# Turning q and k of eight attention heads by VectorE blocks and 128-byte load pieces instead of by TensorE transposes

## The chip, the cores and the metric

One core of a Trainium2 chip runs the whole program. The metric is the device time of one execution in microseconds (us). Five engines work in parallel, each with its own in-order queue: TensorE (PE; its weight loads are shown apart as PEld), VectorE (DVE), ScalarE (ACT), GpSimd (POOL) and SyncE (SP). SP and POOL issue most of the DMA transfers.

## The reference

One layer over 512 tokens of width 1024 in fp32: an RMS norm, one input projection, three token mixers (pooling, a gated linear recurrence "RG-LRU", and stick-breaking attention with 8 heads of 128), gates, a merge, an output projection, and a SwiGLU feed-forward block. Cut to what the change touches:

```python
h = rms_norm(x, norm_mix)
u_pool, u_lru, q, k, v, g_logits = jnp.split(h @ w_in, splits, axis=-1)

# RG-LRU gates, xb = the convolved u_lru in 16 blocks of 64
r = sigmoid(einsum('bshi,hij->bshj', xb, w_rg) + b_rg)
i = sigmoid(einsum('bshi,hij->bshj', xb, w_ig) + b_ig)

# attention: norm over each head's 128 columns, then scores
qh = rms_norm(q.reshape(B, S, 8, 128), q_norm)   # y * rsqrt(mean(y*y) + EPS) * g
kh = rms_norm(k.reshape(B, S, 8, 128), k_norm)
for each block of 128 queries (end = its last row):
    z = einsum('bqhd,bkhd->bhqk', qh_block, kh[:, :end]) * 128 ** -0.5
    log_keep = where(causal, log_sigmoid(-z), 0)
    after = reverse_cumsum(log_keep) - log_keep
    w = where(causal, exp(log_sigmoid(z) + after), 0)
    y = einsum('bhqk,bkhd->bqhd', w, vh[:, :end])
```

## The kernel before

**Products.** Every fp32 product runs as three fp32r passes on PE: high part times high part, high times low, low times high (`mm3`, L304 to 308; `product`, L310 to 317, in a seven-product scheme). A weight tile of 128x1024 is loaded as `raw` (or `qw`), ACT copies it to its high part `whi` (L141), and DVE subtracts to get the low part `wlo` (L142). There are three buffers each for raw, whi and wlo, and SP's next weight load (L148) waits until the wlo of an older raw is done. PE starts a 512-column matmul about every 0.21 us.

**Order.** The program is written as stages with side tasks between the products (`step`, `tick`, and the list `bg`), and a scheduler sets each engine's queue from the order in the code, from raised priorities (`tc.high_priority`) and from explicit places (`tc.issue_after`). Each engine then works through its queue in that order.

**Stages.** In time: the RMS norm and the first gates; the LRU's products with convolution, gates and scan in four chunks, beside more gates; the v, k and q products (`tok_product`, L828 its matmuls); the gates of the third branch; the pool chunks with the attention heads as side tasks; the branch projections, the merge, the output projection, the feed-forward block.

**LRU gates.** For each chunk c, `conv` builds xc, `split` writes its high part xch and its low part xcl (L650), and `gates(0)`, `gates(1)` run three passes each into one PSUM tile `lg`: xch with the high weights lwh, xcl with lwh, xch with the low weights lwl (L660). Each pass is a pair of matmuls on 64 rows.

**q, k, v.** The products leave blocks of 256 tokens by 512 columns: `snap` copies PSUM to an SBUF tile r (ACT, L841), `final` adds the second product (DVE, L849), and `post` ends the block. For q and k, ACT squares the 128x1024 tile (L788, L794) and DVE sums each 128 columns (L789, L795); q's sums go to `qss` and are used as scales of the scores later; k's sums become a reciprocal root `krs`, and `post2` scales r with it in eight ACT steps (L807). `store` (POOL's DMA, L781) puts the block into a DRAM tensor qd.

**Heads.** `head_tasks(h)` gives eight tasks. `load` (SP, L1068) fetches q, k and v of the head into `at` tiles, 128 partitions (tokens) x 4 x 128, as 512-byte pieces. `trans` turns q and k so that the head's 128 columns lie on partitions: four PE transposes each into a PSUM tile `pq` (L1075), from which ACT writes the high part `qkh` (L1079), DVE the low part `qkl` (L1080), and ACT an fp32 copy `f` of the first 128 (L1083). `scores` makes z in three groups; the first 128x128 block is one fp32 product of the two f (L1101), the others are `mm3`. Sigmoids (K, A on ACT), a scan (DVE), transposes of the weights w (`wtrans`, PE, tile `pw`) and the product with v (`yout`, tile `py`) follow.

Of the kernel before, what the change touches and what calls it, by code (L numbers as in the profile page):

```python
# [64 lines left out]
def layer_kernel(ctx: ExitStack, tc: tile.TileContext, x, xt, vecs, w_in, w_qkv7, w_gate7, w_pool, w_rg, w_ig,  # L65
# [371 lines left out]
    with ExitStack() as first:  # L437
# [131 lines left out]
        def lru_constants():  # L569
            dve.tensor_scalar(qg, vcol("q_norm"), QSCALE, None, ALU.mult)  # L570
# [58 lines left out]
        def lru_chunk(c):  # L629
# [17 lines left out]
            def split():  # L647
                st["h"], st["l"] = b4([2, S], f"xch{c}", "b", F32R), b4([2, S], f"xcl{c}", "b", F32R)
                dve.tensor_copy(st["h"], xc)
                dve.tensor_tensor(st["l"], xc, st["h"].bitcast(F32), ALU.subtract)  # L650
# [3 lines left out]
            def gates(j):  # L654
                ct = 2 * c + j
                ps = pb.tile([P, 2, S], F32, tag="mm", name=f"lg{c}{j}")
                for n, (w, x_) in enumerate((("h", "h"), ("h", "l"), ("l", "h"))):
                    for n2 in range(2):
                        q = LH[n2]
                        nc.tensor.matmul(ps[:, n2, :], lw[w][q, ct, :], il(st[x_][q, j, :]),  # L660
                                         start=n == 0, stop=n == 2)
                for n2 in range(2):
                    q, o = LH[n2], LH[1 - n2]
                    act(two(st["r"][q, j, :]), in_order(ps[q, n2, :]), AF.Tanh, scale=0.5, bias=brg[q, ct:ct + 1])
                    act(two(st["i"][q, j, :]), in_order(ps[o, n2, :]), AF.Tanh, scale=0.5, bias=bigx[o, ct:ct + 1])

            def tanh():
                st["t"] = b4([2, S], f"lt{c}")
                dve.scalar_tensor_tensor(st["i"], st["i"], 1.0, xc, ALU.add, ALU.mult)
# [9 lines left out]
            def both():  # L679
                gates(0)  # L680
                gates(1)

            return lambda: early(conv), lambda: early(split), both, tanh
# [68 lines left out]
        def step(*fs):  # L752
            bg.append(lambda: [f() for f in fs])
# [3 lines left out]

        c0, s0, g0, t0 = lru_chunk(0)
# [8 lines left out]
        step(c3), step(s3), step(of(lru_decay, 1), of(lru_scan, 0)), step(t2, of(lru_input, 1))  # L767
# [16 lines left out]
        def post(t, i, j, r):  # L784
            if t < 2:
                sq = b4([2, 512], f"sq{t}{i}{j}")
                if t == 0:
                    act(sq, r, AF.Square)  # L788
                    dve.tensor_reduce(qss[:, 2 * j:2 * j + 2, 4 * i:4 * i + 4],  # L789
                                      sq.rearrange("p a (b d) -> p a b d", d=HD), AX.X, ALU.add)  # L790
                    store(t, i, j, r)
                    return
# [5 lines left out]
            if t == 2:  # L798
                store(t, i, j, r)
# [966 lines left out]
```

## Time and profile before

| what | value |
|---|---|
| three runs | 866.56, 866.76, 868.84 us; median 866.76 |
| the profiled execution | 866.14 us, span 864.3 us, granted clock 0.999 |
| PE / PEld busy | 857.8 / 788.8 us |
| DVE / ACT / POOL busy | 732.3 / 527.0 / 88.8 us |
| DMA packets | 116643, of these 8160 under 512 bytes |

The span is the time between the first and the last instruction of the execution. Busy time is summed per engine; a row of the groups shows the line of the code, the engine, the output and input tiles, the shape, how many, the busy time in us, the mean of one in ns, and the idle time before it with what ended it. SPq is SP's own queue, where DMA issues are counted.

### The profile page before, as it was taken

To read this page: it belongs to the slowest core of one execution; us is meant where nothing else is said; L and a number is where in the kernel's file an instruction comes from. 1 tells how busy PE (TensorE), PEld (TensorE's weight loads), DVE (VectorE), ACT (ScalarE), POOL (GpSimd) and SP (SyncE) were. 2 spreads that over 40 slices of the span, in tenths; PEclk is the share of its full clock that TensorE was granted. 3 is DMA by queue.
4 is the path that set the end of the run, shared out by engine and by line. 5 is a ranking of instruction groups with operands and counts; after the bars stand their busy time and mean duration, and the time that the engine had idled before them with its cause. 6 is when DMAs were issued, how large, how long until landed. Compare 5 with 4: busy or idle time off the path is not lost.

```text
span 864.3 us, 14239 instructions
## 1 busy us (share of the span) xinstructions
PE 857.8 (99%) x5547; PEld 788.8 (91%) x5547; DVE 732.3 (85%) x937; ACT 527.0 (61%) x751; POOL 88.8 (10%) x128
## 2 busy tenths in 40 slices
PE   9999999999999999999999999999999999999998
PEld 7888878888899988889989988889999999999998
DVE  7899897998796598967897787699988888899974
ACT  7554989556966567556665545465555555755642
POOL 1110002132432101000001100000000000121200
PEclk9999999999999999999999999999999999999999
DMA  9586346799592766745737955345533433798913
GB/s 336 169 287 206 101 152 186 224 319 264 172 306 83 234 205 213 226 118 157 242 93 176 200 167 177 100 140 141 163 105 98 123 98 125 224 243 206 192 38 122
DMA packets 116643, 154.08 MB, mean 178 GB/s; under 512 B 8160, under 2 KB 90080, under 8 KB 116576
## 3 DMA queue, kind: packets, MB, share of 16 engines
q1 hardware_dynamic: 103904, 107.30, 39.1%
q0 software_dynamic: 12528, 45.62, 22.4%
q8 instruction: 43, 0.70, 0.3%
q10 hardware_dynamic: 144, 0.26, 0.1%
q14 instruction: 24, 0.20, 0.1%
HBM read 132.71 MB, written 18.87 MB: 175 GB/s over the span
## 4 chain that ended last, share of the span: by engine, by line
PE 92%; ACT 4%; DVE 2%; issue 1%; DMA 0%; SPq 0%; DVEq 0%; ACTq 0%
PE ps_y L315 11%; PE ps_q L828 8%; PE ps_x L315 8%; PE ps_dy L1685 6%; PE ps_dx L1685 5%; PE ps_br L308 3%; PE ps_br L306 3%; PE ps_br L307 3%; PE ps_gate L731 3%; PE ps_bY L1309 2%; PE ps_gy L315 2%; PE ps_bX L1309 2%; PE ps_gx L315 2%; PE ps_pool L306 2%; PE ps_pool L308 2%; PE ps_pool L307 2%
## 5 line engine op out<-in xcount | busy, mean ns | idle before, releaser
L141 ACT ACTIVATE whi<-raw 128x1024 fp32r<-128x1024 f32 x69 | 72.8, 1055 | 75.8 <-PE ps_out L307 16.0
L142 DVE TENSOR_TENSOR wlo<-raw,whi 128x1024 fp32r<-128x1024 f32 x69 | 84.2, 1220 | 25.8 <-ACT whi L141 25.1
L142 DVE TENSOR_TENSOR wlo<-qw,whi 128x1024 fp32r<-128x1024 f32 x48 | 58.4, 1219 | 16.5 <-ACT whi L141 16.5
L141 ACT ACTIVATE whi<-qw 128x1024 fp32r<-128x1024 f32 x48 | 50.3, 1052 | 26.2 <-PE ps_q L828 11.8
L1470 ACT ACTIVATE wh_S<-w_S 128x1024 fp32r<-128x1024 f32 x36 | 38.3, 1063 | 28.7 <-PE ps_y L315 20.1
L1591 POOL DMA_DIRECT2D dw<-in_w_down_dram x20 | 16.9, 862 | 305.1 <-DVE wl L1471 242.9
L1471 DVE TENSOR_TENSOR wl_S<-w_S,wh_S 128x1024 fp32r<-128x1024 f32 x36 | 43.8, 1219 | 3.3 <-ACT wh_S L1470 3.3
L1470 ACT ACTIVATE wh<-w 128x1024 fp32r<-128x1024 f32 x27 | 28.7, 1061 | 27.7 <-PE ps_x L315 9.4
L1471 DVE TENSOR_TENSOR wl<-w,wh 128x1024 fp32r<-128x1024 f32 x27 | 32.9, 1219 | 7.9 <-ACT wh L1470 7.9
L1470 ACT ACTIVATE whdS<-dw 128x1024 fp32r<-128x1024 f32 x20 | 21.3, 1064 | 20.9 <-PE ps_dy L1685 10.6
L1118 DVE TENSOR_TENSOR_SCAN E<-K,ahead 128x512 f32<-128x512 f32 (+3 forms) x32 | 25.3, 812 | 6.2 <-ACT K L1114 6.2
L1471 DVE TENSOR_TENSOR wldS<-dw,whdS 128x1024 fp32r<-128x1024 f32 x20 | 24.2, 1220 | 5.4 <-ACT whdS L1470 5.4
L306 PE MATMUL ps_br<-yph,whi 128*128 128x512 f32 x64 | 24.6, 385 | 0.0
L306 PE MATMUL ps_lru<-HH,whi 128*128 128x512 f32 x64 | 24.6, 384 | 0.0
L306 PE MATMUL ps_pool<-HH,whi 128*128 128x512 f32 x64 | 24.5, 383 | 0.0
L306 PE MATMUL ps_br<-yHH,whi 128*128 128x512 f32 x64 | 24.5, 383 | 0.0
L306 PE MATMUL ps_gate<-HH,whi 128*128 128x512 f32 x64 | 24.4, 381 | 0.0
L307 PE MATMUL ps_br<-yHL,whi 128*128 128x512 f32 x64 | 24.3, 379 | 0.0
L308 PE MATMUL ps_lru<-HH,wlo 128*128 128x512 f32 x64 | 24.3, 379 | 0.0
L307 PE MATMUL ps_gate<-HL,whi 128*128 128x512 f32 x64 | 24.3, 379 | 0.0
L307 PE MATMUL ps_pool<-HL,whi 128*128 128x512 f32 x64 | 24.3, 379 | 0.0
L308 PE MATMUL ps_pool<-HH,wlo 128*128 128x512 f32 x64 | 24.3, 379 | 0.0
(745 smaller groups left out, 3427.2 us busy)
## 6 DMA issues: line engine op xcount, KB each, us to landing
raw<-in_w_in_dram SPq DMA_DIRECT2D x31, 512.0 KB, 5.3
qw<-in_w_qkv_dram SPq DMA_DIRECT2D x24, 512.0 KB, 7.7
dw<-in_w_down_dram POOLq DMA_DIRECT2D x20, 512.0 KB, 8.5
w<-in_w_ffn_gate_dram SPq DMA_DIRECT2D x36, 256.0 KB, 4.0
w<-in_w_ffn_up_dram SPq DMA_DIRECT2D x36, 256.0 KB, 4.6
raw<-in_w_branch_dram SPq DMA_DIRECT2D x16, 512.0 KB, 4.1
qw<-in_w_qkv_dram POOLq DMA_DIRECT2D x12, 512.0 KB, 8.5
qd<-r POOLq DMA_DIRECT2D x12, 512.0 KB, 7.3
```

The costliest lines, as they stand in the source:

```text
L141: act(hi, raw, AF.Copy)
L142: los.append(dve.tensor_tensor(lo, raw, hi.bitcast(F32), ALU.subtract).ins)
L306: nc.tensor.matmul(ps, lh, rh, start=start, stop=False, skip_group_check=skip)
L307: nc.tensor.matmul(ps, lh, rl, start=False, stop=False, skip_group_check=skip)
L308: nc.tensor.matmul(ps, ll, rh, start=False, stop=stop, skip_group_check=skip)
L315: nc.tensor.matmul(o, a_[a][:, w, k, :], il2(b_[b][:, k, :]), start=first and n == k == 0, stop=last and n == 2 and k == 3, skip_group_che ...
L731: nc.tensor.matmul(pss[n // 2][n % 2], w[:, k % 2, n * P:(n + 1) * P], il(hu[k][x_]), start=k == 0 and w is wh and x_ == 0, stop=k == KT - ...
L828: nc.tensor.matmul(ps[:, a, :], b_[:, k, ts_], il(a_[:, kk, :]), start=first and n == k == 0, stop=n == 2 and k == 3, skip_group_check=True)
L1309: nc.tensor.matmul(o, ah[x_][:, w, k, :], il2(b[k][y_]), start=first_ and n == k == 0, stop=n == 2 and k == 3, skip_group_check=True)
L1470: act(h, src, AF.Copy)
L1471: dve.tensor_tensor(l, src, h.bitcast(F32), ALU.subtract)
L1685: nc.tensor.matmul(o, a_[a][:, w, k0 + k, :], il2(b_[b][:, k, :]), start=first and i == k == 0, stop=last and i == 2 and k == nk - 1, skip ...
```

## The change

- `turn`: DVE transposes each 128x1024 tile of q and k in 32x32 blocks (into the tile that held the squares), and that is stored. `load` fetches q and k of a head in four DMAs each; a DMA takes 512 pieces of 32 elements (128 bytes) and puts each block where the turned tile wants it. v is loaded as before. The PE transposes into pq and that tile are gone; `trans` reads the loaded tile.
- Squares: eight ACT operations of 128x128 with `accum_out` (each followed by reading the accumulator) in place of one of 128x1024 and DVE's sum.
- `k_norm` is folded into q's factor qg, so k needs no factor and its f is the loaded tile itself. The first block of z, and what reads it, is in plain instead of interleaved column order, as is the product with `wtf`. A tile "gap" and a wider f only move addresses.
- LRU gates: both PSUM tiles of a chunk are filled together, the passes that read xcl last. On DVE, `behind_lo(3)` puts chunk 3's xcl ahead of li and of `lru_input(1)`.
- q's block (1, 0) is finished later: its squares in the first part of the third branch's gates, its transpose and store in the second.

```diff
-            dve.tensor_scalar(qg, vcol("q_norm"), QSCALE, None, ALU.mult)
+            dve.scalar_tensor_tensor(qg, vcol("q_norm"), QSCALE, vcol("k_norm"), ALU.mult, ALU.mult)
...
-                dve.tensor_tensor(st["l"], xc, st["h"].bitcast(F32), ALU.subtract)
+                st["lo"] = dve.tensor_tensor(st["l"], xc, st["h"].bitcast(F32), ALU.subtract).ins
...
-            def gates(j):
-                ct = 2 * c + j
-                ps = pb.tile([P, 2, S], F32, tag="mm", name=f"lg{c}{j}")
-                for n, (w, x_) in enumerate((("h", "h"), ("h", "l"), ("l", "h"))):
+            def gates():
+                ps = [pb.tile([P, 2, S], F32, tag="mm", name=f"lg{c}{j}") for j in range(2)]
+                for js, passes in (((0, 1), (("h", "h", True, False), ("l", "h", False, False))),
+                                   ((0, 1), (("h", "l", False, True),))):
+                    for j in js:
+                        for w, x_, start, stop in passes:
+                            for q in LH:
+                                nc.tensor.matmul(ps[j][:, LH.index(q), :], lw[w][q, 2 * c + j, :],
+                                                 il(st[x_][q, j, :]), start=start, stop=stop)
+                for j in range(2):
...
-                dve.scalar_tensor_tensor(st["i"], st["i"], 1.0, xc, ALU.add, ALU.mult)
+                with behind_lo(3) if c == 2 else nullcontext():
+                    dve.scalar_tensor_tensor(st["i"], st["i"], 1.0, xc, ALU.add, ALU.mult)
...
+        def behind_lo(c):
+            return tc.issue_after(lru[c]["lo"])
...
+        def behind_input():
+            with behind_lo(3):
+                lru_input(1)
...
-        step(c3), step(s3), step(of(lru_decay, 1), of(lru_scan, 0)), step(t2, of(lru_input, 1))
+        step(c3), step(s3), step(of(lru_decay, 1), of(lru_scan, 0)), step(t2, behind_input)
...
         def post(t, i, j, r):
-            if t < 2:
-                sq = b4([2, 512], f"sq{t}{i}{j}")
-                if t == 0:
-                    act(sq, r, AF.Square)
-                    dve.tensor_reduce(qss[:, 2 * j:2 * j + 2, 4 * i:4 * i + 4],
-                                      sq.rearrange("p a (b d) -> p a b d", d=HD), AX.X, ALU.add)
-                    store(t, i, j, r)
-                    return
-                s_ = cst.tile([P, 8], F32, tag="ssq", name=f"ssq{t}{i}{j}", bufs=2)
-                act(sq, r, AF.Square)
-                dve.tensor_reduce(s_, sq.rearrange("p a (b d) -> p (a b) d", d=HD), AX.X, ALU.add)
-                dve.tensor_scalar(s_, s_, 1.0 / HD, EPS, ALU.mult, ALU.add)
-                bg.append(lambda: post2(t, i, j, r, s_))
             if t == 2:
                 store(t, i, j, r)
-
-        def post2(t, i, j, r, s_):
-            y = cst.tile([P, 8], F32, tag="krs", name=f"krs{i}{j}", bufs=2)
-            rsqrt(y.rearrange("p (a b) -> p a b", a=2), s_.rearrange("p (a b) -> p a b", a=2), (2, 4),
-                  f"q{t}{i}{j}")
-            v = r.rearrange("p a (b d) -> p (a b) d", d=HD)
-            for n in range(8):
-                act(v[:, n, :], v[:, n, :], AF.Copy, scale=y[:, n:n + 1])
-            store(t, i, j, r)
+                return
+            z = b4([2, 512], f"sq{t}{i}{j}")
+            sums = qss[:, 2 * j:2 * j + 2, 4 * i:4 * i + 4] if t == 0 else cst.tile(
+                [P, 2, 4], F32, tag="ssq", name=f"ssq{t}{i}{j}", bufs=2)
+            for a in range(2):
+                for n in range(4):
+                    cs = slice(n * HD, (n + 1) * HD)
+                    act(z[:, a, cs], r[:, a, cs], AF.Square, accum_out=sums[:, a, n:n + 1])
+            if t == 0 and i > j:
+                state["last"] = lambda: turn(t, i, j, r, z)
+                return
+            if t == 0:
+                turn(t, i, j, r, z)
+                return
+            dve.tensor_scalar(sums, sums, 1.0 / HD, EPS, ALU.mult, ALU.add)
+            bg.append(lambda: post2(t, i, j, r, z, sums))
+
+        def turn(t, i, j, r, z):
+            dve.transpose(z.rearrange("p a c -> p (a c)"), r.rearrange("p a c -> p (a c)"))
+            store(t, i, j, z)
+
+        def post2(t, i, j, r, z, s_):
+            y = cst.tile([P, 2, 4], F32, tag="krs", name=f"krs{i}{j}", bufs=2)
+            rsqrt(y, s_, (2, 4), f"q{t}{i}{j}")
+            for a in range(2):
+                for n in range(4):
+                    v = r[:, a, n * HD:(n + 1) * HD]
+                    act(v, v, AF.Copy, scale=y[:, a, n:n + 1])
+            turn(t, i, j, r, z)
...
-                if (t, key) != (0, (0, 0)):
+                if (t, key) == (0, (1, 0)):
+                    state["last"] = lambda v=r[key]: post(0, 1, 0, v)
+                elif (t, key) != (0, (0, 0)):
                     bg.append(lambda t=t, key=key, v=r[key]: post(t, *key, v))
...
+                if (cc, nm) == (0, "S4"):
+                    state["last"]()
+                if (cc, nm) == (1, "S1"):
+                    with tc.issue_after(los[-1]):
+                        state["last"]()
...
+        ap1.tile([P, 72], F32, tag="gap", name="gap")
...
-                        r = (ex.tile([P, NS, HD], F32, tag="u", name=f"at{h}{t}") if h == 0 and t < 2
-                             else slot_ld(f"at{h}{t}", (NS, HD)))
-                        nc.sync.dma_start(r, qd[t, g][:, hd].rearrange("(b p) c -> p b c", p=P))
+                        shape = (NS, HD) if t == 2 else (S,)
+                        r = (ex.tile([P] + list(shape), F32, tag="u", name=f"at{h}{t}") if h == 0 and t < 2
+                             else slot_ld(f"at{h}{t}", shape))
+                        if t == 2:
+                            nc.sync.dma_start(r, qd[t, g][:, hd].rearrange("(b p) c -> p b c", p=P))
+                        else:
+                            src = qd[t, g].rearrange("(b j) (c i) -> c j b i", j=32, i=32)
+                            for c in range(4):
+                                nc.sync.dma_start(r[32 * c:32 * c + 32].rearrange("p (b i) -> p b i", i=32),
+                                                  src[4 * j + c])
...
-                for t, gcol in ((0, qg), (1, vcol("k_norm"))):
-                    pt = paux.tile([P, S], F32, tag="aux", name=f"pq{h}{t}")
-                    for s in range(NS):
-                        nc.tensor.transpose(pt[:, s * P:(s + 1) * P], st["raw", t][:, s, :], idn)
+                for t in range(2):
+                    raw = st["raw", t]
                     a = slot_r(f"qkh{h}{t}")
                     b = slot_r(f"qkl{h}{t}")
-                    c = slice(0 if t else P, S)
-                    act(a[:, c], pt[:, c], AF.Copy, scale=gcol)
-                    dve.scalar_tensor_tensor(b[:, c], pt[:, c], gcol, a[:, c].bitcast(F32), ALU.mult, ALU.subtract)
+                    if t:
+                        act(a, raw, AF.Copy)
+                        dve.tensor_tensor(b, raw, a.bitcast(F32), ALU.subtract)
+                        st["f", t] = raw[:, 0:P]
+                    else:
+                        c = slice(P, S)
+                        act(a[:, c], raw[:, c], AF.Copy, scale=qg)
+                        dve.scalar_tensor_tensor(b[:, c], raw[:, c], qg, a[:, c].bitcast(F32), ALU.mult,
+                                                 ALU.subtract)
+                        st["f", t] = f = ap1.tile([P, 96 + P], F32, tag="f", name=f"f{h}")[:, 96:]
+                        act(f, raw[:, 0:P], AF.Copy, scale=qg)
                     st[t] = (a, b)
-                    st["f", t] = f = ap1.tile([P, P], F32, tag=f"f{t}", name=f"f{h}{t}")
-                    act(f, pt[:, 0:P], AF.Copy, scale=gcol)
...
-                        nc.tensor.matmul(z[:, c0:c0 + n], st["f", 0], il(st["f", 1], 64), start=True, stop=True)
+                        nc.tensor.matmul(z[:, c0:c0 + n], st["f", 0], st["f", 1], start=True, stop=True)
...
-                    zs = in_order(z[:, cs], 64)
-                    act(two(K[:, cs], 64), zs, AF.Sigmoid, scale=qrs[:, 1, i, h:h + 1])
-                    act(two(A[:, cs], 64), zs, AF.Sigmoid, scale=qrs[:, 0, i, h:h + 1])
+                    zs, Ki, Ai = z[:, cs], K[:, cs], A[:, cs]
+                    if i:
+                        zs, Ki, Ai = in_order(zs, 64), two(Ki, 64), two(Ai, 64)
+                    act(Ki, zs, AF.Sigmoid, scale=qrs[:, 1, i, h:h + 1])
+                    act(Ai, zs, AF.Sigmoid, scale=qrs[:, 0, i, h:h + 1])
```

PE at an LRU chunk's gates. Before:

```order
L308 MATMUL ps_lru_720<-HH_107,wlo_690 128x512
L660 MATMUL lg_787<-xch_681,lwh 128x512 x2
L660 MATMUL lg_787<-xcl_682,lwh 128x512 x2
L660 MATMUL lg_787<-xch_681,lwl 128x512 x2
L660 MATMUL lg_798<-xch_681,lwh 128x512 x2
L660 MATMUL lg_798<-xcl_682,lwh 128x512 x2
L660 MATMUL lg_798<-xch_681,lwl 128x512 x2
L306 MATMUL ps_lru_720<-HH_107,whi_689 128x512
```

In the changed kernel:

```order
L308 MATMUL ps_lru_720<-HH_107,wlo_690 128x512
L661 MATMUL lg_787<-xch_681,lwh 128x512 x2
L661 MATMUL lg_787<-xch_681,lwl 128x512 x2
L661 MATMUL lg_788<-xch_681,lwh 128x512 x2
L661 MATMUL lg_788<-xch_681,lwl 128x512 x2
L661 MATMUL lg_787<-xcl_682,lwh 128x512 x2
L661 MATMUL lg_788<-xcl_682,lwh 128x512 x2
L306 MATMUL ps_lru_720<-HH_107,whi_689 128x512
```

The two pairs that read xcl stand behind all four that read xch.

DVE around the low part of the last chunk (xcl_1079). Before:

```order
L142 TENSOR_TENSOR wlo_1132<-raw_1129,whi_1131 128x1024
L649 CAST xch_1078<-xc_1032 128x1024
L669 SCALAR_TENSOR_TENSOR li_898<-li_898,xc_825 128x1024
L650 TENSOR_TENSOR xcl_1079<-xc_1032,xch_1078 128x1024
L706 SCALAR_TENSOR_TENSOR ls_976<-lr_767,ls_976 128x1024
```

In the changed kernel:

```order
L142 TENSOR_TENSOR wlo_1132<-raw_1129,whi_1131 128x1024
L649 CAST xch_1078<-xc_1032 128x1024
L650 TENSOR_TENSOR xcl_1079<-xc_1032,xch_1078 128x1024
L675 SCALAR_TENSOR_TENSOR li_898<-li_898,xc_825 128x1024
L711 SCALAR_TENSOR_TENSOR ls_976<-lr_767,ls_976 128x1024
```

xcl has moved one place forward, ahead of li.

ACT in the k products, where whi is the split of the next weight tile, r<-ps_q the copy of a finished product, and sq the squares. Before:

```order
L141 ACTIVATE whi_1854<-qw_1573 128x1024
L841 ACTIVATE r_1852<-ps_q_1643 128x1024
L794 ACTIVATE sq_1858<-r_1811 128x1024
L141 ACTIVATE whi_1891<-qw_1575 128x1024
L141 ACTIVATE whi_1913<-qw_1795 128x1024
L794 ACTIVATE sq_1920<-r_1772 128x1024
L141 ACTIVATE whi_1953<-qw_1797 128x1024
L141 ACTIVATE whi_1974<-qw_1835 128x1024
L794 ACTIVATE sq_1978<-r_1852 128x1024
L141 ACTIVATE whi_2011<-qw_1837 128x1024
L841 ACTIVATE r_2027<-ps_q_1973 128x1024
```

In the changed kernel:

```order
L141 ACTIVATE whi_1861<-qw_1573 128x1024
L857 ACTIVATE r_1859<-ps_q_1643 128x1024
L803 ACTIVATE sq_1865,ssq_1866<-r_1818 128x128 x2
L141 ACTIVATE whi_1905<-qw_1575 128x1024
L803 ACTIVATE sq_1865,ssq_1866<-r_1818 128x128 x6
L141 ACTIVATE whi_1927<-qw_1802 128x1024
L803 ACTIVATE sq_1934,ssq_1935<-r_1779 128x128 x5
L141 ACTIVATE whi_1974<-qw_1804 128x1024
L803 ACTIVATE sq_1934,ssq_1935<-r_1779 128x128 x3
L141 ACTIVATE whi_1995<-qw_1842 128x1024
L803 ACTIVATE sq_1999,ssq_2000<-r_1859 128x128 x5
L141 ACTIVATE whi_2039<-qw_1844 128x1024
```

Each single square has become two to six short ones between two splits.

SP where the loads of heads 1 and 2 (at) stand among the pool's and the branch's weights (raw). Before:

```order
L1068 DMA at_2752<-qd_88 128x4x128
L1068 DMA at_2903<-qd_84 128x4x128
L1068 DMA at_2905<-qd_86 128x4x128
L1068 DMA at_2907<-qd_88 128x4x128
L148 DMA raw_2918<-in_w_in_dram 128x4x256
L148 DMA raw_2972<-in_w_in_dram 128x4x256
L1068 DMA at_3080<-qd_84 128x4x128
L1068 DMA at_3082<-qd_86 128x4x128
L1068 DMA at_3084<-qd_88 128x4x128
L148 DMA raw_3052<-in_w_in_dram 128x4x256
```

In the changed kernel, from head 0's v on:

```order
L1094 DMA at_2815<-qd_88 128x4x128
L1098 DMA at_2954<-qd_84 32x16x32
L1098 DMA at_2959<-qd_86 32x16x32
L148 DMA raw_2975<-in_w_in_dram 128x4x256
L148 DMA raw_3029<-in_w_in_dram 128x4x256
L1094 DMA at_2964<-qd_88 128x4x128
L1098 DMA at_2954<-qd_84 32x16x32
L148 DMA raw_3097<-in_w_in_dram 128x4x256
L1098 DMA at_2959<-qd_86 32x16x32 x2
L148 DMA raw_3181<-in_w_branch_dram 128x4x256
L1098 DMA at_2954<-qd_84 32x16x32
L1098 DMA at_2959<-qd_86 32x16x32
```

Three loads of a head in a row have become nine, spread between weight loads.

PE in the last head, where z waits for the low parts (qkl), among products of the branch (ps_br). Before:

```order
L306 MATMUL z_0_4333<-qkh_4265,qkh_4254 128x512
L306 MATMUL ps_br_1_1_4230<-yph_3606,whi_4125 128x512
L307 MATMUL ps_br_1_1_4230<-ypl_3607,whi_4125 128x512
L307 MATMUL z_0_4333<-qkl_4266,qkh_4254 128x512
L308 MATMUL z_0_4333<-qkh_4265,qkl_4255 128x512
L308 MATMUL ps_br_1_1_4230<-yph_3606,wlo_4126 128x512
```

In the changed kernel the same two passes stand here:

```order
L306 MATMUL ps_br_2_1_4414<-yph_3370,whi_4254 128x512
L307 MATMUL z_0_4342<-qkl_4277,qkh_4270 128x512
L308 MATMUL z_0_4342<-qkh_4276,qkl_4271 128x512
L307 MATMUL z_1_4399<-qkl_4277,qkh_4270 128x384
L308 MATMUL z_1_4399<-qkh_4276,qkl_4271 128x384
L307 MATMUL ps_br_2_1_4414<-ypl_3371,whi_4254 128x512
```

They have moved from the third place behind z's first pass to some forty rows behind it.

23 lines of the change are left out of this document (10 added, 13 removed).

## The prediction

> **What bounds the kernel now.** I read the page first: the busy shares (part 1), then the chain that ended last (part 4).
>
> ```profile
> PE 857.8 (99%) x5547; PEld 788.8 (91%) x5547; DVE 732.3 (85%) x937; ACT 527.0 (61%) x751; POOL 88.8 (10%) x128
> PE 92%; ACT 4%; DVE 2%; issue 1%; DMA 0%; SPq 0%; DVEq 0%; ACTq 0%
> ```
>
> TensorE (PE) is busy for 857.8 of 864.3 us, and the chain lies on it for 92%. So time is won by taking work off PE's queue or by closing one of its few gaps, and lost by making PE wait; what other engines do counts only through that. Next come the waits of PE (us in total, times, longest):
>
> ```profile
> PE lg L660 <- DVE xcl L650: 1.3, 1, 1.3
> PE z L307 <- DVE qkl L1080: 0.5, 1, 0.5
> PE ps_q L828 <- DVE wlo L142: 0.2, 1, 0.2
> ```
>
> The first two are in code that the change rewrites. The third is at the q, k, v products, where ScalarE gets more to do. A time above the sum below would have to appear as such a row.
>
> **The change part by part.**
>
> *64 PE transposes go.* The group, from the view by line and shape, and the timeline of PE around the first head's eight (start, length):
>
> ```profile
> L1075 PE MATMUL pq<-idn,at 128*128 128x128 f32 x64 | 8.3, 273 | 0.0
> 297.12 0.38 PE L308 MATMUL ps_pool<-HH,wlo 128*128 128x512 f32 x1
> 297.33 1.04 PE L1075 MATMUL pq<-idn,at 128*128 128x128 f32 x8
> 298.13 0.46 PE L306 MATMUL ps_pool<-HH,whi 128*128 128x512 f32 x1
> 298.43 0.38 PE L307 MATMUL ps_pool<-HL,whi 128*128 128x512 f32 x1
> ```
>
> Matmuls overlap, so I count starts, not lengths. A 512-column product takes 0.21 us (297.12 to 297.33). The eight begin at 297.33, and the second product behind them begins at 298.43: 1.10 us, of which one product's 0.21 remains. So a head's eight cost 0.88 us, the dearer step after them (0.30) included. Eight heads: 8 x 0.88 = 7.0 us, all on the path. This is the main term.
>
> *LRU gates reordered.* PE around its one long wait, and VectorE (DVE) at the same place:
>
> ```profile
> 120.83 0.48 PE L660 MATMUL lg<-xch,lwh 64*128 64x512 f32 x2
> 122.66 0.48 PE L660 MATMUL lg<-xcl,lwh 64*128 64x512 f32 x2 [1.34 <-DVE xcl L650]
> 122.98 0.38 PE L660 MATMUL lg<-xch,lwl 64*128 64x512 f32 x2
> 119.66 0.68 DVE L649 CAST xch<-xc 128x1024 fp32r<-128x1024 f32 x1
> 120.26 1.21 DVE L669 SCALAR_TENSOR_TENSOR li<-li,xc 128x1024 f32<-128x1024 f32 x1
> 121.39 1.21 DVE L650 TENSOR_TENSOR xcl<-xc,xch 128x1024 fp32r<-128x1024 f32 x1
> ```
>
> DVE now does xcl ahead of li, so xcl would end at 120.26 + 1.21 = 121.5. PE has four pairs to do before it needs xcl: a first step of 0.32 (as 122.66 to 122.98) and three of about 0.21, to 121.8. The wait falls to nothing: 1.3 us. What is late next is li, 1.2 us later on DVE; its readers are DVE's own rows behind it, not PE. The range of this term is -1.3 to 0.
>
> *The wait for qkl, 0.5 us.* In the last head PE now issues the passes that read k's low part some forty matmuls later, so I count -0.5, with 0 as the other end, since a new wait may stand there.
>
> *Squares: eight of 128x1024 become 64 of 128x128 that also sum.* From the groups, and ScalarE's (ACT) timeline at the only summing squares that the kernel has now:
>
> ```profile
> L794 ACT ACTIVATE sq<-r 128x1024 f32<-128x1024 f32 x4 | 4.2, 1058 | 4.0 <-DVE r L849 4.0
> L788 ACT ACTIVATE sq<-r 128x1024 f32<-128x1024 f32 x4 | 4.2, 1054 | 1.6 <-DVE r L849 1.6
> L807 ACT ACTIVATE r<-r,krs 128x128 f32<-128x128 f32 x32 | 10.3, 388 | 2.6 <-DVE krs L346 2.5
> L511 ACT ACTIVATION_READ_ACCUMULATOR xs<-xs 128x1 f32 x8 | 1.5, 186 | 0.0
> 16.45 0.63 ACT L511 ACTIVATE xs<-xs 128x512 f32<-128x512 f32 x1
> 16.99 0.19 ACT L511 ACTIVATION_READ_ACCUMULATOR xs<-xs 128x1 f32 x1
> 17.08 0.61 ACT L511 ACTIVATE xs<-xs 128x512 f32<-128x512 f32 x1
> 225.23 1.04 ACT L141 ACTIVATE whi<-qw 128x1024 fp32r<-128x1024 f32 x1
> 226.17 1.85 ACT L807 ACTIVATE r<-r,krs 128x128 f32<-128x128 f32 x6
> ```
>
> No 128x128 square with a sum is in the trace. The lower end is a plain 128x128 operation, 0.30 us in a run of overlapping ones (six in 1.85 us, the last 0.39 long); reading the sum adds 17.08 - 16.99 = 0.09, some 0.4 us together. The upper end is both lengths without overlap, 388 + 186 = 574 ns. I take 0.41, because the timeline shows the overlap. A block's eight then take 3.3 us instead of 1.06: over eight blocks 26.2 - 8.4 = +18 us of ACT (at the upper end 36.7 - 8.4 = +28). The cover is ACT's idle time there; the windows (PE, PEld, DVE, ACT, POOL busy):
>
> ```profile
> 190.00:285.00 95.00, 95.00 (x594) 87.11 (x594) 74.75 (x85) 68.20 (x97) 30.37 (x28) 1.00 0.67 196
> 220.00:240.00 20.00, 20.00 (x93) 17.02 (x93) 15.09 (x22) 17.61 (x36) 6.41 (x6) 1.00 0.58 180
> ```
>
> ACT has 27 us free in 95, so 18 fit in sum, with little left at 220 to 240 (2.4 of 20). Each weight tile (whi, split by ACT) feeds 12 products, 12 x 0.21 = 2.6 us, and with three buffers ACT may be about one tile, 2.6 us, late before PE stands still. Between two whi the new order puts up to six squares: 6 x 0.41 + 0.94 (whi's own step, 225.23 to 226.17) = 3.4 us, late by 0.8; two such tiles in a row, 1.6. That is inside the cover, but narrowly. At 0.57 a square six take 3.4 + 0.94 = 4.4, late by 1.8 a tile; two tiles in a row 3.6, which is 1.0 past the cover, for each of eight blocks 8 us. Ends 0 and +8; I take +1.5, near the lower one.
>
> *DVE: eight sums out, eight block transposes in.*
>
> ```profile
> L789 DVE TENSOR_REDUCE qss<-sq 128x8 f32<-128x1024 f32 x4 | 4.9, 1214 | 0.0
> L795 DVE TENSOR_REDUCE ssq<-sq 128x8 f32<-128x1024 f32 x4 | 4.9, 1213 | 0.0
> ```
>
> 9.7 us go. The trace has no transpose on DVE. Between the cheapest 128x1024 form, the 0.68-us cast above, and twice the common 1.21 lies what it may cost; I take 1.21, that of nearly every fp32 operation of this size, so the net is nothing. At 2.4 each DVE gains 9.7 us: 84 of 95, still not the bound, but a wlo could come up to a microsecond late twice: +2. The Trainium skill, "VectorE: DVE Perf Modes", The three transpose paths, gives 311 ns for a 128x128 bf16 block on VectorE and 390 on TensorE, and its rules advise TensorE for 128x128; by 311, an estimate is 2.5 us for the eight in 128x1024, and the sum would be some 861. No run so far shows it.
>
> *Per head.* ACT loses k's 128x128 copy f, and both splits read SBUF instead of PSUM; ACT and DVE have the slack for either sign (15.15 and 17.95 busy of 26 in the window 284 to 310 below). The un-interleaved first block of z has the same columns on PE: 0.
>
> *Loads.* 16 loads of 512-byte pieces become 64, each with as many pieces (512) of 128 bytes. The issues of the loads now, those of the one load of 256-byte pieces that the kernel has (also 512 each), q1's packets, the two windows that price them (the columns before the rate: granted clock, DMA share), and who holds SP and the weight split:
>
> ```profile
> L1068 SPq DMA_DIRECT2D at<-qd x24: 359/458/1456, 252.7 to 400.5; - x24
> L618 SPq DMA_DIRECT2D rawl<-in_w_rg_dram x2: 630/642/654, 29.3 to 30.0; - x2
> q1 hardware_dynamic: 103904, 107.30, 39.1%
> 26.00:34.00 8.00, 8.00 (x43) 7.12 (x42) 5.98 (x9) 2.49 (x3) 0.00 (x0) 1.00 0.74 197
> 38.00:40.00 2.00, 2.00 (x11) 1.76 (x10) 2.00 (x3) 2.00 (x4) 0.00 (x0) 1.00 0.98 353
> 284.00:310.00 26.00, 26.00 (x142) 23.30 (x141) 17.95 (x25) 15.15 (x24) 2.82 (x6) 1.00 0.98 286
> SPq L148 <- DVE wlo L142: 207.5, 44, 30.0
> ACT whi L141 <- PE ps_pool L307: 10.2, 7, 3.7
> ```
>
> SP: 64 x 0.64 - 16 x 0.46 = +34 us of issuing between 284 and 400, against a queue that over the span spends 207.5 us waiting for weight buffers. What queues behind a piece is the next raw load.
>
> Transfer time, as an estimate: 26 to 34 us moved 8 x 197 KB = 1.58 MB in 0.74 x 8 = 5.9 us of all engines: two 512-KB weight loads (at 353/0.98 = 360 GB/s, 2.9 us) and four gate loads of 128 KB, so 3.0 us for 2048 packets of 256 bytes, 23.5 ns on one engine. All of q1: 0.391 x 864.3 x 16 / 103904 = 52 ns for 1033 bytes on average. A line through both gives 14 ns plus 0.037 per byte: 18.8 ns for 128 bytes, 32.9 for 512. A head's q and k (8 loads, 4096 pieces) then take 4.8 us instead of 2.1 (1024 pieces). Three heads load at 284 to 310, where the DMA is full (0.98): +8 us there. The cover is the three raw buffers: a tile feeds 24 products, 5.2 us, so 15.6 us, and ACT's split waits there for PE, not for a load. Net 0. The ends are 0 and, at 52 ns a piece, (13.3 - 2.1) x 3 - 15.6 = +18.
>
> **Sum** against the profiled execution, 866.14 us (span 864.3 and 1.8 around it): 866.14 - 7.0 - 1.3 - 0.5 + 1.5 = 858.8. The median of the three runs, 866.76, lies 0.6 above it, so I forecast 859.4, or -0.85%.
>
> **Rivals.**
>
> *Small pieces starve PE (slower).* Place: 284 to 345, where heads 1 to 3 load between the pool's weights. For it: a full DMA there, four times the issues, and raw loads queued behind pieces on SP. Against: the 256-byte row. It decides from the piece's price: the stall eats the remaining 7.3 us when 3 x (4096p/16 - 2.1) - 15.6 = 7.3, at p = 38 ns, twice my estimate. At two 256-byte packets' time, 47 ns, the stall is 14 us: 866.14 - 7.3 + 14 = 873. The rule beside it: the Trainium skill, "DMA: Bandwidth & Descriptors", Specifications, wants at least 512 B for line rate and says that below this the engine does a read-modify-write; by it the 47 ns and 873 would be the reading. The 256-byte loads at 23.5 ns agree that small packets are dear per byte, but not that they are dearer than long ones. Chance 0.10.
>
> *ACT becomes the bound in the k and q products.* At 0.57 a square, +8: 866.14 - 8.8 + 8 = 865.3, no measurable change. For it: 17.61 of 20 at 220 to 240. Chance 0.12.
>
> *The transposes' time turns into waits for the loads.* ACT's qkh now stands directly behind the DMA, ahead of a whi in its queue; were each head's pieces some 0.8 us too late, PE would wait about what it transposed: 865. Head 1's loads now, the landing times of all, and head 1's first use:
>
> ```profile
> 290.54 4.04 SPq L1068 DMA_DIRECT2D at<-qd  x4
> DMA to landing us min/median/max: 2.7/6.2/10.6
> 312.57 1.04 PE L1075 MATMUL pq<-idn,at 128*128 128x128 f32 x8
> ```
>
> Against it: issued by 294.6 and landed 10.6 later at the latest, head 1's are there 7 us ahead of use, and head 0's were asked for at 252.7. Chance 0.10.
>
> *Slow block transposes on DVE*, +2: 861. Chance 0.08.
>
> **How the numbers follow.** The forecast itself, 857 to 862, has 0.60. A measurement here tells about 0.3% (2.6 us) from no change, so faster means below 864.2. Faster: 0.60 + 0.08, and 0.08 from milder forms of the two at 865: 0.76. Same: the rest of these, 0.14. Slower: 0.10. The range is 857 to 868: it holds the forecast, both 865s and small stalls beyond, and leaves out the starved case.
>
> **What would show it.** No pq rows; PE busy near 850; no lg wait; PE waits for wlo at ps_q below 2 us in total (more means the ACT case); 64 accumulator squares stepping 0.41; STREAM_TRANSPOSE near 1.2; packets under 512 B near 41,000, and no ACT or PE wait on at or raw at 284 to 345 (one of over 5 us means the starved case). If the products' step around a removed block isn't 0.21, the main term is wrong.

## The result: 858.79 us, 0.88% faster

| | before | changed |
|---|---|---|
| median (range) | 866.67 us (866.56 to 868.84, 4 runs) | 858.79 us (858.54 to 859.57, 4 runs) |
| ratio, 95% interval | | 0.9912 [0.9899, 0.9925] |
| profiled execution, span | 866.14 us, 864.3 us | 858.89 us, 856.8 us |

The forecast was 859.4. Two more series of the changed kernel, run as a measure for the experiments, gave 859.95 (ratio 0.9925 [0.9913, 0.9937]) and 859.81 (0.9915 [0.9901, 0.9929]).

The profile after: busy shares, the chain, the DMA packets.

```profile
PE 850.3 (99%) x5483; PEld 781.2 (91%) x5483; DVE 732.3 (85%) x937; ACT 533.3 (62%) x863; POOL 88.6 (10%) x128
PE 88%; ACT 4%; DVE 4%; issue 3%; POOL 1%; DMA 0%; DVEq 0%; POOLq 0%
DMA packets 141988, 154.09 MB, mean 180 GB/s; under 512 B 41696, under 2 KB 115424, under 8 KB 141920
```

PE has 64 matmuls and 7.5 us less and is still busy for 99%. DVE's time is unchanged, ACT has 6 us more. 33536 more packets are under 512 bytes. What PE waits for now (total, times, longest):

```profile
PE ps_q L844 <- DVE wlo L142: 1.5, 4, 0.5
PE warm_ps L451 <- DVE warm L328: 1.1, 1, 1.1
PE ps_gate L736 <- DVE lt L587: 0.4, 1, 0.4
PE ps_q0S L844 <- DVE wlo L142: 0.2, 1, 0.2
```

The waits for xcl and for qkl are gone, and the 0.2 us for wlo have become 1.7, at the v and q products. The groups that the prediction priced without a row:

```profile
L803 ACT ACTIVATE sq<-r 128x128 f32<-128x128 f32 x64 | 18.8, 298 | 2.5 <-DVE r L865 2.5
L803 ACT ACTIVATION_READ_ACCUMULATOR sq<-r 128x1 f32 x64 | 12.2, 190 | 0.0
L814 DVE STREAM_TRANSPOSE sq<-r 128x1024 f32<-128x1024 f32 x8 | 9.9, 1241 | 0.5 <-ACT r L823 0.5
L1136 PE MATMUL z<-at,f 128*128 128x128 f32 x16 | 3.1, 275 | 0.0
L1186 PE MATMUL py<-wtf,at 128*128 128x128 f32 x16 | 3.1, 275 | 0.0
188.18 0.31 ACT L803 ACTIVATE sq<-r 128x128 f32<-128x128 f32 x1 [0.20 <-DVE r L865]
188.40 0.19 ACT L803 ACTIVATION_READ_ACCUMULATOR sq<-r 128x1 f32 x1
188.49 0.30 ACT L803 ACTIVATE sq<-r 128x128 f32<-128x128 f32 x1
```

A small square with its sum steps 0.30 us (188.18 to 188.49), not 0.41. A DVE transpose takes 1.24 us, like a common operation of that size.

**Where PE gained and lost.** The same matmul can be found in both traces, and the difference of its two start times is the lead of the changed kernel. I set the lead to zero before the last LRU gates and read it at later places. Two such pairs, at the first pool product and at the first product of the merge (first and last start), before and then changed:

```profile
L306 PE MATMUL ps_pool<-HH,whi x64: 379/379/463, 287.0 to 340.6; 128*128 128x512 f32 x64
L1309 PE MATMUL ps_bY<-B11h,whi x16: 272/275/275, 466.3 to 484.7; 128*128 128x256 f32 x16
```

```profile
L306 PE MATMUL ps_pool<-HH,whi x64: 379/379/382, 287.6 to 338.4; 128*128 128x512 f32 x64
L1347 PE MATMUL ps_bY<-B11h,whi x16: 273/275/275, 458.7 to 477.1; 128*128 128x256 f32 x16
```

At the pool's start the changed kernel is 0.6 us behind (0.1 of it there from the first); by the merge it is 7.6 ahead. The lead in us, at the time of the kernel before, for all kernels (labels below):

| kernel | 126, LRU gates done | 187, v done, in k | 221, in q | 250, q done | 346, branches begin | 400 | 470, merge |
|---|---|---|---|---|---|---|---|
| changed | 1.6 | 0.3 | 0.4 | -0.5 | 2.3 | 5.2 | 7.7 |
| after_again | 1.6 | 0.3 | 0.4 | -0.6 | 2.2 | 4.5 | 7.0 |
| after_third | 1.6 | 0.3 | 0.4 | -0.4 | 2.3 | 3.9 | 6.4 |
| no_transposes | 0.0 | 0.0 | 0.0 | 0.1 | 2.7 | 4.4 | 6.0 |
| lru_only | 1.6 | 0.3 | 0.4 | 0.7 | 0.7 | -0.6 | -0.6 |
| plain_order | 0.0 | 0.0 | 0.0 | 0.0 | 0.2 | -0.3 | -0.1 |
| pieces_only | 0.0 | 0.0 | 0.0 | 0.1 | 0.1 | -0.3 | -0.3 |
| no_lru | 0.0 | 0.0 | -0.1 | -1.6 | 1.2 | 3.1 | 5.6 |
| whole_squares | 1.6 | 0.3 | 0.4 | 0.2 | 2.9 | 5.2 | 7.7 |
| whole_squares_again | 1.6 | 0.3 | 0.4 | 0.2 | 2.9 | 4.7 | 7.2 |
| late_tail | 1.6 | -2.1 | -2.3 | -3.6 | -0.9 | 0.8 | 3.3 |
| turn_twice | 1.6 | 0.3 | 0.4 | -1.9 | 0.1 | 1.8 | 4.3 |
| pieces64 | 1.6 | 0.3 | 0.4 | -0.6 | 2.2 | 1.9 | 4.4 |

Between repeats of one kernel the columns up to 346 agree within 0.15 us; the column at 400 doesn't, by up to 1.3. So up to 346 us the table tells apart effects that the times alone leave inside their intervals.

### The profile page after: what moved, and what is told of

It reads as the page before. It is cut to its first block, busy times and chain, and to the rows that moved or that the text cites. A ratio compares the mean times of both kernels' runs of the same rounds, so it can differ in the third digit from the quotient of the medians.

```text
span 856.8 us, 14307 instructions
## 1 busy us (share of the span) xinstructions
PE 850.3 (99%) x5483; PEld 781.2 (91%) x5483; DVE 732.3 (85%) x937; ACT 533.3 (62%) x863; POOL 88.6 (10%) x128
## 4 chain that ended last, share of the span: by engine, by line
PE 88%; ACT 4%; DVE 4%; issue 3%; POOL 1%; DMA 0%; DVEq 0%; POOLq 0%
PE ps_y L315 11%; PE ps_x L315 8%; PE ps_dy L1723 6%; PE ps_q L844 5%; PE ps_dx L1723 5%; PE ps_br L306 3%; PE ps_br L307 3%; PE ps_br L308 3%; PE ps_bY L1347 3%; PE ps_gy L315 3%; PE ps_gate L736 2%; PE ps_bX L1347 2%; PE ps_gx L315 2%; PE ps_pool L308 2%; PE ps_pool L306 2%
## 5 line engine op out<-in xcount | busy, mean ns | idle before, releaser
L142 DVE TENSOR_TENSOR wlo<-qw,whi 128x1024 fp32r<-128x1024 f32 x48 | 58.3, 1220 | 11.6 <-ACT whi L141 11.2
L1509 DVE TENSOR_TENSOR wl<-w,wh 128x1024 fp32r<-128x1024 f32 x27 | 32.9, 1220 | 8.2 <-ACT wh L1508 8.2
L307 PE MATMUL ps_br<-ypl,whi 128*128 128x512 f32 x64 | 24.3, 380 | 0.0
L307 PE MATMUL ps_lru<-HL,whi 128*128 128x512 f32 x64 | 24.3, 379 | 0.0
L308 PE MATMUL ps_gate<-HH,wlo 128*128 128x512 f32 x64 | 24.3, 379 | 0.0
```

Of the source, the lines that this page charges most:

```text
L142: los.append(dve.tensor_tensor(lo, raw, hi.bitcast(F32), ALU.subtract).ins)
L307: nc.tensor.matmul(ps, lh, rl, start=False, stop=False, skip_group_check=skip)
L308: nc.tensor.matmul(ps, ll, rh, start=False, stop=stop, skip_group_check=skip)
L1509: dve.tensor_tensor(l, src, h.bitcast(F32), ALU.subtract)
```

## The experiments

**The transposes alone.** Edit on the kernel before:

```diff
-                    pt = paux.tile([P, S], F32, tag="aux", name=f"pq{h}{t}")
-                    for s in range(NS):
-                        nc.tensor.transpose(pt[:, s * P:(s + 1) * P], st["raw", t][:, s, :], idn)
+                    pt = st["raw", t].rearrange("p a c -> p (a c)")
```

This kernel leaves the turning of q and k out altogether, so its scores are of unturned data.

> The kernel before with the 64 PE transposes of q and k left out; the splits read the loaded tile as it lies, so the scores are of unturned data. Loads, squares, LRU gates and fp32 products as before. Main theory (PE's queue is the path, a transposed head costs 0.88 us of it): -7.0 us from the transposes and up to -0.5 from the wait for qkl, so 859.2 to 859.8. Rival (the transposes' time turns into waits for loads or splits): 863 or more, with new PE waits at z.

Measured: 859.69 us (859.48 to 861.49) against 866.37, ratio 0.9924 [0.9909, 0.9939]: -6.7 us, with no turned load, block transpose or small square in it. The waits of PE:

```profile
PE ps_br L307 <- DMA yHL<-ydl: 0.7, 1, 0.7
PE z L307 <- DVE qkl L1078: 0.5, 1, 0.5
```

The main theory holds: 6.7 us are 0.84 us a head. The wait for qkl stayed, so taking the transposes out doesn't remove it. Another came: at 351 us in the time of the kernel before, where the branch reads the LRU's low part (yHL) from a load that POOL issues late (its row follows below).

**The LRU order alone.** Edit on the kernel before: the `gates`, `behind_lo` and `behind_input` parts of the change.

> The kernel before with the new order of the LRU gates and of chunk 3's low part alone. Main theory: PE's 1.3-us wait for xcl goes, and the first v products start 1.5 us earlier, but DVE, full there with the LRU's tail, gives the low parts wlo at about the same absolute time as before, so PE's lead is eaten by waits for wlo before 165 us: 866.2 to 866.8, no change. Rival (the sum of the prediction): the lead lasts to the end, 865.2 to 865.5.

Measured: 865.71 us (864.88 to 866.85, 11 runs), ratio 0.9992 [0.9983, 1.0001]. By time neither theory is excluded. The trace tells: 1.6 us won at the gates, 0.3 left after v, 0.7 at 250 us. (The profiled execution took 866.70 us, among the slowest of the 11; the wait for yHL below is in it.) The waits, and those of the changed kernel's v products in its timeline, with DVE's load there (the windows give PE, PEld, DVE, ACT, POOL busy) before and changed:

```profile
PE ps_q L837 <- DVE wlo L142: 1.2, 3, 0.5
PE ps_br L307 <- DMA yHL<-ydl: 1.1, 1, 1.1
```

```profile
143.95 0.48 PE L844 MATMUL ps_q<-wlo,HH 128*128 128x512 f32 x1 [0.29 <-DVE wlo L142]
147.35 0.48 PE L844 MATMUL ps_q<-wlo,HH 128*128 128x512 f32 x1 [0.55 <-DVE wlo L142]
160.93 0.48 PE L844 MATMUL ps_q<-wlo,hT3h 128*128 128x512 f32 x1 [0.36 <-DVE wlo L142]
```

```profile
138.00:162.00 24.00, 23.77 (x111) 20.49 (x110) 22.86 (x21) 18.77 (x22) 4.01 (x6) 1.00 0.61 161
```

```profile
138.00:162.00 24.00, 22.80 (x104) 19.02 (x103) 24.00 (x23) 17.89 (x20) 5.05 (x7) 1.00 0.61 158
```

PE arrives 1.5 us earlier, but DVE, with the end of the LRU in its queue, is busy for 24.00 of 24 us and gives the low parts hardly earlier: 1.2 us of the gain turn into waits for wlo. In this execution the rest goes at yHL. That load waits for PE's last pool product and then for the DMA:

```profile
341.49 0.54 POOL L1225 DMA_DIRECT2D yHL<-ydl  x1 [7.26 <-PE ps_pool L308]
```

This is the kernel before; PE needs the tile at 351.7, 10 us later, and the loads of yHL land 5.2 to 9.7 us after issue there, up to 10.5 in lru_only. It is the wait that differs between the repeats of the changed kernel: none in the first trace, 0.3 and 1.0 us in the other two, in the order of their leads at 400 us, and of the slowest landing of a yHL load (8.3, 9.1 and 9.8 us). What makes the landing vary was not tried.

**The plain column order alone.** Edit on the kernel before: `il(st["f", 1], 64)` and `il(wtf, 64)` read plain, and the ACT copies around them as in the change.

> The kernel before with only the column order of the fp32 products changed: the first block of z and the product with wtf read and write plain order. Main theory: each fp32 product costs PE 0.04 to 0.05 us less in plain order (300 against 275 ns a row), 16 products, so -0.7 us: 866.0, and the mean of the rows L1101 and L1148 is 275. Rival (the lengths of the rows are only modelled, or follow from something else in the changed kernel): no change and rows near 300.

Measured: 865.88 us (865.41 to 867.04, 11 runs), ratio 0.9992 [0.9984, 1.0001]. The rows fell from 300 to 275 ns as expected:

```profile
L1101 PE MATMUL z<-f,f x16: 272/275/275, 309.2 to 440.3; 128*128 128x128 f32 x16
309.20 0.38 PE L1101 MATMUL z<-f,f 128*128 128x128 f32 x2
309.34 0.41 PE L306 MATMUL z<-qkh,qkh 128*128 128x384 f32 x1
309.59 0.33 PE L307 MATMUL z<-qkl,qkh 128*128 128x384 f32 x1
```

From the fp32 product to the second pass behind it 0.39 us pass (309.20 to 309.59), where the kernel before took 0.43 (309.22 to 309.65). The lead grows by 0.16 up to 346 us and by 0.37 from 356 to 470; between them the wait for yHL (0.4 us) takes more than that away. So the effect is there, some 0.5 us of the 0.7 expected, but the time alone doesn't show it.

**128-byte pieces alone.** Edit on the kernel before:

```diff
-                        nc.sync.dma_start(r, qd[t, g][:, hd].rearrange("(b p) c -> p b c", p=P))
+                        src = qd[t, g][:, hd].rearrange("(b p) c -> p b c", p=P)
...
+                            for c in range(4):
+                                cc = slice(32 * c, 32 * c + 32)
+                                nc.sync.dma_start(r[:, :, cc], src[:, :, cc])
```

> The kernel before with each load of q and k in four DMAs of 128-byte pieces, into the same places; nothing else changed. Main theory: DMA and SP have room, 866.2 to 867.2, no PE wait for at or raw, DMA share between 280 and 430 us higher by about 0.04. Rival (small pieces starve the weights): some us slower, with waits of ACT for raw or of PE for at.

Measured: 865.93 us (865.69 to 866.92), ratio 0.9994 [0.9985, 1.0003]. The windows of 280 to 430 us, before, with the pieces, and in the changed kernel (the last columns: clock, DMA share, GB/s):

```profile
280.00:430.00 150.00, 150.00 (x821) 134.49 (x821) 120.46 (x186) 93.93 (x184) 8.83 (x16) 1.00 0.65 197
```

```profile
280.00:430.00 150.00, 149.83 (x817) 134.09 (x817) 120.19 (x186) 93.64 (x182) 8.83 (x16) 1.00 0.71 197
```

```profile
280.00:430.00 150.00, 149.96 (x800) 134.21 (x799) 124.62 (x198) 94.25 (x183) 7.88 (x15) 1.00 0.69 193
```

The same bytes take 0.06 x 150 = 9 us more of all 16 engines, and no PE wait for at or raw appears. With 32.9 ns for a 512-byte piece, the line's value, 28672 small pieces in place of 7168 come to (9 x 16000 + 7168 x 32.9) / 28672 = 13 ns each, an estimate. The packet records of the trace agree: the 28672 packets of 128 bytes in this window take 13.2 ns on average. The rival is out at this size.

**64-byte pieces.** Edit on the changed kernel: each of the four DMAs of a load is made as two, of 16 elements a piece.

> The changed kernel with 64-byte pieces: each of the 64 loads of q and k as two DMAs, 128 DMAs and 65536 pieces. Main theory (a piece costs one DMA engine some 11 to 13 ns, and neither the engines nor SP's queue is the bound): DMA share between 280 and 430 us up by about 0.13 to 0.8, SP issues 31 us more, the time within 1 us of the changed kernel. Rival (twice the pieces reach the limit and starve the weights or delay q and k): 3 us or more slower, with PE or ACT waits for at or raw.

Measured: 861.15 us (861.07 to 861.86) against 859.81 beside it, ratio to before 0.9939 [0.9924, 0.9953]: 1.3 us slower than the changed kernel in its median. Its waits of PE, of ACT, and the window:

```profile
PE ps_br L307 <- DMA yHL<-ydl: 1.2, 1, 1.2
PE ps_br L306 <- DMA yHH<-ydh: 0.5, 2, 0.3
ACT whi L141 <- DMA raw<-in_w_branch_dram: 3.5, 1, 3.5
280.00:430.00 150.00, 147.82 (x782) 131.17 (x782) 121.45 (x190) 93.09 (x182) 7.88 (x15) 1.00 0.79 187
```

The share is 0.79, as expected; neither theory's time is met. The lead falls from 2.2 to 1.9 between 346 and 400 us, where the changed kernel gains 1.6 to 2.9. The first loads that PE misses are the LRU's, not the heads'; besides these PE stands 0.4 us at the pool's products (for DVE's p21l), and the 3.5 us that a weight split waits for its load end in no wait of PE. So at twice the pieces, in twice the DMAs, the loads begin to cost. Which of the two it is was not tried apart.

**The changed kernel again, and without the LRU part** (its `split`, `gates`, `tanh` and `step` lines as before).

> The changed kernel once more, as the measure for the three beside it: 858.3 to 859.2.

> The changed kernel with the LRU gates and chunk 3's low part in the order of before. Main theory: the 1.3-us wait for xcl is back, but the waits for wlo at the first v products (1.2 us up to 161 us) go in exchange, so the time stays within 0.5 us of the changed kernel, 858.6 to 859.3. Rival (the reorder gives its 1.3 us): 860.0 to 860.4.

Measured: after_again 859.95 us (859.13 to 861.89); no_lru 860.74 us (860.25 to 861.26), ratio to before 0.9932 [0.9920, 0.9944]. The times lie 0.8 apart with intervals that overlap; in the trace no_lru is 1.0 us behind at 250 us (-1.6 against -0.6). This lies between the two theories, and mine falls: I took the gain for gone after v. With the LRU part 0.4 us are left at 221 us, and without it the stall in the q products behind that is larger (0.8 us, where the changed kernel has 0.3):

```profile
PE lg L660 <- DVE xcl L650: 1.3, 1, 1.3
PE ps_q L835 <- DVE wlo L142: 1.0, 2, 0.8
```

**The squares of before in the changed kernel.** Edit:

```diff
-            for a in range(2):
-                for n in range(4):
-                    cs = slice(n * HD, (n + 1) * HD)
-                    act(z[:, a, cs], r[:, a, cs], AF.Square, accum_out=sums[:, a, n:n + 1])
+            act(z, r, AF.Square)
+            dve.tensor_reduce(sums, z.rearrange("p a (b d) -> p a b d", d=HD), AX.X, ALU.add)
```

> The changed kernel with the squares of before: one ACT square of 128x1024 and one DVE sum a block, then the DVE transpose. Main theory: the 0.7 to 0.9 us that PE loses between 220 and 250 us come from whi, late behind the 64 small squares on ACT; they go, 857.9 to 858.2, though DVE gets 9.7 us more in 95 and may put a new wait for wlo there. Rival (they come from DVE, which now also turns the tiles): no gain or slower, 859 to 861, with the waits for wlo at ps_q longer.

> The changed kernel, as the measure for the three beside it: 858.5 to 860.2.

> The changed kernel with the squares and sums of before, a second time, since 858.99 against 859.95 is within the intervals. Main theory (the small squares on ACT hold up whi at 220 to 240 us and cost PE 0.65 us): 0.5 to 1.0 us below the changed kernel beside it, and again a lead of 0.6 us more at 240 us in the trace. Rival (the difference was chance): equal within 0.3 us, the trace's lead gone.

Measured: 858.99 us (858.47 to 860.11) against 859.95, then 859.34 (857.64 to 859.75) against 859.81 (858.29 to 859.96). Both medians are lower, by 1.0 and 0.5 us, with overlapping intervals (ratios to before 0.9913 [0.9900, 0.9926] and 0.9910 [0.9897, 0.9923]). The lead at 250 us is 0.2 both times, against -0.6 and -0.4: 0.6 to 0.7 us. The windows of 190 to 285 us, before, changed, and with whole squares (the second series):

```profile
190.00:285.00 95.00, 95.00 (x594) 87.11 (x594) 74.75 (x85) 68.20 (x97) 30.37 (x28) 1.00 0.67 196
```

```profile
190.00:285.00 95.00, 94.49 (x587) 86.18 (x586) 74.86 (x83) 76.63 (x207) 29.91 (x28) 1.00 0.69 194
```

```profile
190.00:285.00 95.00, 94.74 (x594) 87.05 (x593) 82.71 (x92) 67.61 (x96) 31.45 (x28) 1.00 0.68 194
```

In this window small squares put 8.4 us on ACT; whole squares put 7.8 us on DVE instead, and cost PE less. So of the change's parts this one cost time, in the trace. Whether the version with whole squares is the faster one isn't shown by the times.

The loss is one stall. ACT ahead of it and PE's wait in the changed kernel, then ACT with whole squares (the second series), where PE has no wait there:

```profile
218.63 1.85 ACT L823 ACTIVATE r<-r,krs 128x128 f32<-128x128 f32 x6
220.39 1.00 ACT L857 ACTIVATE r<-ps_q 128x1024 f32<-128x1024 f32 x1
221.29 1.05 ACT L141 ACTIVATE whi<-qs 128x1024 fp32r<-128x1024 f32 x1
223.66 0.48 PE L844 MATMUL ps_q<-wlo,hT2h 128*128 128x512 f32 x1 [0.29 <-DVE wlo L142]
```

```profile
217.94 1.02 ACT L855 ACTIVATE r<-ps_q 128x1024 f32<-128x1024 f32 x1 [0.73 <-PE ps_q L842]
218.86 1.05 ACT L141 ACTIVATE whi<-qs 128x1024 fp32r<-128x1024 f32 x1
219.81 0.98 ACT L821 ACTIVATE r<-r,krs 128x128 f32<-128x128 f32 x3
```

The whi from which that wlo is made begins 2.4 us later with small squares. Only 0.5 us of this are the squares' own length (five end 1.48 us after the first begins, where the whole one took 0.97). The first of them begins 1.0 us later, after a wait for DVE's r, and six scalings of k (1.76 us) stand ahead of this whi that stand behind it with whole squares and in the kernel before. So the order of ACT's queue, which came out otherwise with the small squares, has a large part in the loss. No run has the one without the other.

**The block transposes twice.** Edit on the changed kernel: the line `dve.transpose(...)` in `turn` stands twice.

> The changed kernel with each of the eight block transposes done twice into the same tile: 9.9 us more of DVE between 185 and 285 us, some 85 of 95 busy. Main theory (DVE has the room there): at most 1 us slower than the changed kernel beside it. Rival (DVE is as near the bound there as at 138 to 187 us): 2 us or more slower, as waits for wlo at ps_q.

Measured: 861.32 us (860.81 to 861.42) against 859.81, ratio to before 0.9937 [0.9921, 0.9953]: +1.5 us in the medians, between the two theories. In the trace the lead is -1.9 instead of -0.4 at 250 us, and 0.1 instead of 2.3 at 346. DVE is busy for 81.53 of the 95 us from 190 to 285, and PE stands at these places (the second lies at 257 us):

```profile
PE ps_q0S L845 <- DVE wlo L142: 1.2, 2, 1.0
PE ps_gy L315 <- ACT gx L935: 0.5, 1, 0.5
```

At 2.5 us a block, DVE would thus have cost some 1.5 to 2.2 us. What the blocks cost at 1.24 us no run shows by itself. Whole squares, where DVE has the sums and the transposes, are at 0.2 at 250 us, and lru_only, where it has the sums alone, at 0.7: a difference of 0.5 us, with other parts of the change in it.

**The end of the LRU later.** Edit on the changed kernel: `if (t, nm) == (VKQ[0], "S3")` becomes `"22"`.

> The changed kernel with the end of the LRU (input 3, the last scans, the stores) begun after the last v product instead of after the fifth: four DVE operations move behind later low parts. Main theory (DVE, full at 138 to 162 us, sets PE's start there): the wait of 0.36 us at 160.9 goes, the two at 144 and 147 us stay, 858.2 to 858.6. Rival (DVE is not the limit there, or the store comes too late for the branch): 858.8 or more.

Measured: 862.53 us (861.53 to 863.37), ratio to before 0.9949 [0.9936, 0.9962]: 2.6 us slower than the changed kernel, a miss. The wait at 161 us stayed, and by 187 the lead was -2.1 instead of 0.3. The moved operations stood behind the wlo of 160.9 already, so they could not free it: the same scan (L717) is ahead of it in both traces. DVE there:

```profile
172.52 1.23 DVE L214 TENSOR_TENSOR qs<-qw,qw 128x1024 f32<-128x1024 f32 x1 [2.58 <-DMA qw<-in_w_qkv_dram]
177.06 2.33 DVE L717 TENSOR_TENSOR_SCAN li<-lt,ls 128x512 f32<-128x512 f32 x2
```

DVE's queue now stands 2.6 us for a load, with the scans behind it, and they meet the low parts later. DVE's busy time alone doesn't set PE's start there; the place of each operation in its queue counts too.

## Why the prediction was right, step by step

- **Transposes, -7.0.** Held: -6.7 us alone. Nor did their time turn into waits for the loads: PE waits for no at and no qkh, and the new loads of q and k, a quarter of the size each, land sooner after their issue (median 3.4 us, where the old ones took 6.2):

```profile
DMA to landing us min/median/max: 1.9/3.4/6.3
```

- **LRU gates, -1.3.** The wait went and 1.6 us were won at the place. The step failed in what came next: I named li as the next late thing, with no reader on PE. It was wlo: 1.2 us came back as waits at the v products, where DVE is full. By the traces at 250 us the part is worth 0.7 us alone and 1.0 in the whole, not 1.3.
- **qkl, -0.5.** No wait for qkl stands in PE's list of the changed kernel. Taking the transposes out alone left it. The new place of the passes removed it, not a faster low part: after z's first pass (427.83 us) k's low part now comes 7.9 us later, where before it came 1.2 later, and the pass that reads it follows at once:

```profile
435.04 0.68 DVE L1109 TENSOR_TENSOR qkl<-at,qkh 128x512 fp32r<-128x512 f32 x1
435.78 0.48 PE L307 MATMUL z<-qkl,qkh 128*128 128x512 f32 x1
```

- **Squares, +1.5.** The engine and the place held (a late whi on ACT, in q). The mechanism held in part: the squares' length alone makes this whi 0.5 us late, and 1.8 us of k scalings came ahead of it, which the prediction didn't have. The size was off: a square steps 0.30 us, not 0.41, the 64 take 20.3 us of ACT instead of 8.4 (11.9 more, not 18), and PE lost 0.6 to 0.7.
- **DVE transposes, 0.** The price held: 1241 ns, and DVE's busy time is unchanged. Whether their place costs PE something stays open (up to 0.5 us, above). By the Trainium skill, "VectorE: DVE Perf Modes", The three transpose paths, the estimate was 2.5 us a block; here it is half of that for fp32, and the measurement decides.
- **Plain order, 0.** Missed: some 0.5 us were won, because an fp32 product takes less time in plain order.
- **Loads, 0.** Held in time. The price of 18.8 ns was too high; it is 13. It was drawn through 23.5 ns for 256 bytes, and the packet records of the kernel before have 18.2 there. The Trainium skill, "DMA: Bandwidth & Descriptors", Specifications, says that below 512 B the engine does a read-modify-write; no run here shows the 47 ns that the prediction set beside it, but at 64 bytes the loads begin to cost.

So the main term was right for its reason, and that the sum came out right to 0.6 us is in part luck. Up to 250 us it has the changed kernel 0.2 us behind (1.5 - 1.3), and the traces have it 0.4 to 0.6 behind: 0.8 to 0.9 us too much for the squares stand against what the LRU's part lost to wlo and q's other stall. From there to the merge the sum has 7.5 us (7.0 + 0.5), and the three traces gain 8.2, 7.6 and 6.8. The plain order adds to that, and the wait for yHL (0, 0.3 and 1.0 us), a term that the prediction didn't have, takes from it.

## What to carry to other kernels

On an engine that is busy for 99%, count the work taken off its queue by start times; that term held. For a wait that is removed, look at who feeds that engine during the next 40 us: if the feeder is full there, the lead turns into waits for it. Compare the start of the same instruction along two traces; it shows gains and losses of half a microsecond that the times can't.

## What the runs showed of the hardware

- The row of an fp32 128-column product on PE is 275 ns long in plain column order and 300 in the interleaved one, and the next products start 0.04 us sooner behind two such rows.
- Reading the accumulator (190 ns) hides behind the next square: a 128x128 square with its sum steps 0.30 us.
- A piece of 128 bytes costs a DMA engine about 13 ns, and one of 64 bytes some 11: the share rose from 0.69 to 0.79 for 57344 pieces in place of 28672 (280 to 430 us), and (28672 x 13 + 0.10 x 150 x 16000) / 57344 = 11 ns. Both are estimates, and the packet records agree: on average 11.2 ns for 64 bytes (pieces64), 13.1 for 128 (the changed kernel), 18.2 for 256 and 29.2 for 512 (the kernel before). Halving a 128-byte piece saves little of its time.
